# A hybrid attention layer's kernel, scheduled with and without the timeline simulation

## The chip, the cores and the metric

The kernel runs on one core of a Trainium2 chip. The metric is the device time of one execution in microseconds (us). A core has five engines with a queue each, which run in order within the queue and wait for one another by semaphores: PE (TensorE, matrix products; the profile lists its weight loads apart as PEld), DVE (VectorE, elementwise work), ACT (ScalarE, copies, casts and activation functions), POOL (GpSimd) and SP (SyncE, which here issues most of the DMAs). SBUF is the core's working memory, PSUM the memory that PE writes its products to.

## The reference

One layer of a decoder: a mixer of three kinds of heads, then an MLP, all in float32, on 512 tokens of width 2048.

```python
def hybrid_layer(x, norm1_w, w_in, ..., w_out, norm2_w, w_up, w_down):
    h = rmsnorm(x, norm1_w)
    proj = h @ w_in
    ...
    y_sb = stick_breaking_attention(heads(sb_q), heads(sb_k), heads(sb_v))   # 6 heads of 128
    y_sc = sc_b * causal_depthwise_conv(sc_c * sc_h, sc_conv_w)              # 4 groups of 128
    y_gdn = gdn_mixer(gdn_qkv, gdn_z, gdn_a, gdn_b, ...)                     # 6 heads of 128
    y = jnp.concatenate([y_sb.astype(x.dtype), y_sc, y_gdn], axis=-1)
    x = x + y @ w_out
    h2 = rmsnorm(x, norm2_w)
    return x + jnp.square(jax.nn.relu(h2 @ w_up)) @ w_down                   # width 8192
...
return rmsnorm(x, final_norm_w)
```

The gated delta rule (GDN) in `gdn_mixer` solves, for each head and each block of tokens, a unit triangular system, and then carries a 128×128 state from block to block:

```python
t_mat = lax.linalg.triangular_solve(eye + m, jnp.broadcast_to(eye, m.shape),
                                    left_side=True, lower=True, unit_diagonal=True)
...
v_new = u_c - w_c @ state
o = q_c @ state + a_c @ v_new
state = state * jnp.exp(gl_c)[..., None, None] + jnp.swapaxes(k_c, -1, -2) @ v_new
```

## The kernel before

**How the products are made.** Each large product is split for precision: an operand x becomes hi (x rounded to fp32r) and lo (x − hi), and a product is three matmuls, hi·hi, hi·lo and lo·hi (`mm3`, lines 107 to 111). A weight tile is therefore loaded (SP's queue), cast by ACT to hi, and subtracted by DVE to lo before PE can use it. For the projections this is `wload` (line 97): raw, whi and wlo are tiles of 128×512 with four buffers each, and one such chunk feeds 12 matmuls of 512 columns in `gemm_chunk` (line 113). For the MLP it is `w_prep` (line 838) with `split` (lines 823 to 825): W has three buffers of 128×1024, and several of the W are first summed by DVE (L842) or by an accumulating DMA of POOL's queue (L848, L858), because both MLP halves use a Strassen-like scheme of seven products (`UP`, `DOWN`, lines 713 and 714).

**The stages.** First the projection of v and of the gates (lines 179 to 320). Then the GDN heads: `gdn_in(h)` makes a head's q, k, v by three projections, a short convolution and SiLU on DVE and ACT, and the block matrices; `gdn_base(h)` inverts the triangular matrices; `gdn_scan(h)` carries the state through four blocks. `gdn_gate` and `sc_group`, projections with little else, are written between them (lines 654 to 680). Then the six attention heads (`sb_qk`, `sb_attn`, lines 684 to 704), the output projection with the second norm (lines 713 to 797), the up half of the MLP in 32 groups (`up_pair`, line 888), whose results h are stored to DRAM (L943), and the down half (`unit`, line 996), which reads them back (L956). The end is the final norm.

**The solve.** In `gdn_base` the inverse of the 32×32 diagonal blocks is a loop on DVE with two operations a step, each reading what the one before wrote; 16 partitions (4 blocks of 4 diagonal pieces) work at a time:

```python
for i in range(31, 0, -1):
    n = 32 - i
    tv = t[:, :i * n].rearrange("p (a b) -> p a b", a=i)
    V.tensor_tensor(out=tv, in0=B[:, 0:i, i:i + 1].broadcast_to([16, i, n]), ...)                    # L436
    V.tensor_tensor(out=Y[:, 0:i, i:32], in0=Y[:, 0:i, i:32], in1=tv, op=ALU.subtract)               # L438
```

Its input and its result go through DRAM (sm, Bq and sy, Xc; SP's queue), and small matmuls, transposes and copies behind it put the full inverse together.

**What sets the order.** The program is written against a tile framework. It records every instruction with its dependencies, and when the `with tile.TileContext(...)` block closes, a scheduler puts each engine's instructions into the order of that engine's queue. Each instruction has a priority, by default its place in the program. `with tc.high_priority(n)` moves those inside n places forward: `WPRIO` = 400 for `wload`, `DPRIO` = 120 for `w_prep`, `APRIO` = 60 for the down half's loads of h, `CPRIO` = 2000 for `gdn_base` and `gdn_scan` (lines 33 to 36, 645 to 652). The scheduler takes, for an engine that is free, the instruction of the highest priority among those that are ready. In this kernel the context is made with `schedule_with_timeline_sim=True` (line 1151): what is free and what is ready follows a simulation of the program's timeline. The order is fixed at compile time; on the chip each queue runs as written.

## Time and profile before

| | us |
|---|---|
| median of 2 runs | 2193.46 (2193.19 to 2193.73) |
| the profiled execution | 2195.19 |
| its span, first to last instruction | 2193.2 |
| HBM read, written | 302.94 MB, 45.48 MB |

The profiled execution is 1.7 us slower than the median of the runs. Its span is 2.0 us shorter than its time. The granted TensorE clock was 0.996 on the mean. In a group of the profile, "L104 DVE TENSOR_TENSOR wlo<-raw,whi ... x98 | 66.9, 683 | 5.7" is: line 104, engine DVE, operation, the tile written and those read, 98 instructions, 66.9 us busy in all, 683 ns each on the mean, and 5.7 us in which the engine stood idle just before them. A row of a view by stretches of time has for each engine its busy time and its instructions in that stretch, and then the mean granted clock, the busy share of the DMA engines and GB/s. A row of waits has the waiting engine and line, what it waited for, the time in all, the times and the longest.

The stages stand in the trace at about these times after the span's start: the first projection to 67 us, the GDN heads from there to 540, the attention heads to 755, the output projection to 913, the up half to 1555 and the down half to the end.

### The profile page before, as it was taken

Reading aid. Unit: us, or ns where it says so; the run is one execution under the profiler, and the core shown is the slowest. Engines: PE = TensorE matmul, PEld = TensorE weight load, DVE = VectorE, ACT = ScalarE, POOL = GpSimd, SP = SyncE. Lnnn points to the kernel's source line nnn. Section 1 sums busy time; section 2 is a strip of 40 time slices with the busy share of each in tenths; the row PEclk is TensorE's granted clock in tenths of the full one; section 3 lists DMA queues with packets and bytes.
Section 4 is the critical chain, followed back from the end, with each engine's and each line's share of the span. In section 5 each row is a group of like instructions: output and inputs, shape, how many; then the busy total and the mean of one; then the engine's idle time right before and its main releaser. Section 6 shows DMA issues by size and latency. Waiting matters only on the chain.

```text
span 2193.2 us, 33146 instructions
## 1 busy us (share of the span) xinstructions
PE 2153.2 (98%) x12698; PEld 1893.1 (86%) x12698; DVE 1695.1 (77%) x2335; ACT 1067.3 (49%) x1621; POOL 150.4 (7%) x203
## 2 busy tenths in 40 slices
PE   9999999999999999999999999999899999999998
PEld 8887787778989888799999999999788888888876
DVE  6689899754656755587788778877888898889884
ACT  6745566333434544444454445444454454445453
POOL 0000000000000011000000000000001000000113
PEclk9999999999999999999999999999999999999999
DMA  6332222222222344656665666666987777777762
GB/s 190 98 98 84 75 79 88 79 91 85 86 81 84 99 152 153 223 165 185 194 191 171 185 193 191 172 186 193 299 268 183 238 221 214 195 235 213 186 197 77
DMA packets 157390, 350.58 MB, mean 160 GB/s; under 512 B 19792, under 2 KB 59856, under 8 KB 157104
## 3 DMA queue, kind: packets, MB, share of 16 engines
q1 hardware_dynamic: 143984, 300.24, 40.6%
q0 software_dynamic: 13248, 48.24, 12.8%
q8 instruction: 99, 1.62, 0.3%
q14 instruction: 59, 0.48, 0.1%
HBM read 302.94 MB, written 45.48 MB: 159 GB/s over the span
## 4 chain that ended last, share of the span: by engine, by line
PE 91%; DVE 5%; DMA 1%; ACT 1%; issue 1%; SPq 0%; ACTq 0%; DVEq 0%
PE mm L110 10%; PE mm L109 10%; PE mm L111 10%; PE pu L111 10%; PE pu L109 10%; PE pu L110 10%; PE pp L110 8%; PE pp L111 8%; PE pp L109 8%; DVE wlo L104 1%; PE mm L274 1%; PE mm L272 1%; PE mm L273 1%; DVE W L825 1%; DVE Yq L438 1%
## 5 line engine op out<-in xcount | busy, mean ns | idle before, releaser
L824 ACT CAST W<-q 128x1024 fp32r<-128x1024 f32 x436 | 455.0, 1051 | 563.4 <-PE pp L111 247.1
L825 DVE TENSOR_TENSOR W<-q,W 128x1024 fp32r<-128x1024 f32 x436 | 530.5, 1225 | 121.6 <-ACT W L824 121.0
L109 PE MATMUL mm<-big,whi 128*128 128x512 f32 x1024 | 404.8, 396 | 1.8 <-DVE tmp L557 1.6
L111 PE MATMUL mm<-big,wlo 128*128 128x512 f32 x1024 | 403.8, 395 | 0.0
L110 PE MATMUL mm<-big,whi 128*128 128x512 f32 x1024 | 403.3, 394 | 0.0
L110 PE MATMUL pp<-W,A 128*128 128x512 f32 x840 | 328.0, 390 | 3.9 <-DVE W L825 3.9
L111 PE MATMUL pp<-W,A 128*128 128x512 f32 x840 | 327.4, 390 | 1.1 <-DVE A L825 1.1
L109 PE MATMUL pp<-W,A 128*128 128x512 f32 x840 | 325.6, 391 | 2.8 <-ACT A L824 2.8
L104 DVE TENSOR_TENSOR wlo<-raw,whi 128x512 fp32r<-128x512 f32 (+1 forms) x292 | 196.3, 674 | 146.5 <-ACT whi L103 133.7
L103 ACT CAST whi<-raw 128x512 fp32r<-128x512 f32 (+1 forms) x292 | 176.5, 605 | 267.6 <-PE mm L110 221.8
L111 PE MATMUL pu<-XS,W 128*128 128x256 f32 x1024 | 288.9, 282 | 1.2 <-DVE W L825 1.2
L109 PE MATMUL pu<-XS,W 128*128 128x256 f32 x1024 | 289.0, 282 | 1.0 <-ACT W L824 0.8
L110 PE MATMUL pu<-XS,W 128*128 128x256 f32 x1024 | 288.6, 282 | 0.0
L109 PEld LDWEIGHTS mm<-big,whi 128*128 128x128 f32 x1024 | 192.8, 188 | 40.6 <-DVE tmp L557 1.8
L111 PEld LDWEIGHTS mm<-big,wlo 128*128 128x128 f32 x1024 | 192.7, 188 | 40.0 <-DVE wlo L104 0.9
L110 PEld LDWEIGHTS mm<-big,whi 128*128 128x128 f32 x1024 | 192.8, 188 | 38.7 <-DVE big L723 0.3
L109 PEld LDWEIGHTS pu<-XS,W 128*128 128x128 f32 x1024 | 193.4, 189 | 2.0 <-ACT W L824 1.6
L111 PEld LDWEIGHTS pu<-XS,W 128*128 128x128 f32 x1024 | 193.4, 189 | 1.7 <-DVE W L825 1.7
L110 PEld LDWEIGHTS pu<-XS,W 128*128 128x128 f32 x1024 | 193.3, 189 | 0.0
L842 DVE TENSOR_TENSOR q<-q 128x1024 f32<-128x1024 f32 x156 | 190.2, 1219 | 2.1 <-DMA q<-in_wd_dram 0.7
L110 PEld LDWEIGHTS pp<-W,A 128*128 128x128 f32 x840 | 158.1, 188 | 38.4 <-DVE W L825 5.6
L109 PEld LDWEIGHTS pp<-W,A 128*128 128x128 f32 x840 | 158.0, 188 | 37.3 <-ACT A L824 4.1
(300 smaller groups left out, 3398.1 us busy)
## 6 DMA issues: line engine op xcount, KB each, us to landing
q<-in_wu_dram SPq DMA_DIRECT2D x128, 512.0 KB
q<-in_wd_dram SPq DMA_DIRECT2D x128, 512.0 KB
raw<-in_wa_dram SPq DMA_DIRECT2D x192, 256.0 KB
hs<-h SPq DMA_DIRECT2D x32, 1024.0 KB
q<-in_wd_dram POOLq DMA_DIRECT2D x60, 512.0 KB, 7.7
ha<-hs SPq DMA_DIRECT2D x56, 512.0 KB
raw<-in_wo_dram SPq DMA_DIRECT2D x64, 256.0 KB
q<-in_wu_dram POOLq DMA_DIRECT2D x32, 512.0 KB, 5.5
```

The costliest lines, as they stand in the source:

```text
L103: S.copy(out=hi[:, :n], in_=raw[:, :n])
L104: V.tensor_tensor(out=lo[:, :n], in0=raw[:, :n], in1=hi[:, :n].bitcast(F32), op=ALU.subtract)
L109: PE.matmul(p, lhsT=lh, rhs=rh, start=first, stop=False, skip_group_check=more)
L110: PE.matmul(p, lhsT=lh, rhs=rl, start=False, stop=False, skip_group_check=more)
L111: PE.matmul(p, lhsT=ll, rhs=rh, start=False, stop=last, skip_group_check=more)
L272: PE.matmul(o, lhsT=xw[k][:, 0, s], rhs=hi[:, ws], start=k == 0 and b % 2 == 0, stop=False)
L273: PE.matmul(o, lhsT=xw[k][:, 0, s], rhs=lo[:, ws], start=False, stop=False)
L274: PE.matmul(o, lhsT=xw[k][:, 1, s], rhs=hi[:, ws], start=False, stop=k == KT - 1 and b % 2 == 1)
L438: V.tensor_tensor(out=Y[:, 0:i, i:32], in0=Y[:, 0:i, i:32], in1=tv, op=ALU.subtract)
L824: S.copy(out=o[:, 0], in_=src)
L825: V.tensor_tensor(out=o[:, 1], in0=src, in1=o[:, 0].bitcast(F32), op=ALU.subtract)
L842: on_v = lambda t, u: V.tensor_tensor(out=t, in0=t, in1=u, op=ALU.add)
```

## The change

The context is made without the timeline simulation. The scheduler orders the instructions by their priorities alone, without its own model of their times. The instructions, their operands, tiles, buffer counts and priorities are the same.

```diff
-    with tile.TileContext(nc, schedule_with_timeline_sim=True) as tc:
+    with tile.TileContext(nc, schedule_with_timeline_sim=False) as tc:
```

## The prediction

> **What bounds the kernel now.** I read the page's first two parts, then busy time by stage, then groups and timeline where the engines are fullest.
>
> ```profile
> span 2193.2 us, 33146 instructions
> PE 2153.2 (98%) x12698; PEld 1893.1 (86%) x12698; DVE 1695.1 (77%) x2335; ACT 1067.3 (49%) x1621; POOL 150.4 (7%) x203
> ...
> PE   9999999999999999999999999999899999999998
> ...
> DVE  6689899754656755587788778877888898889884
> ...
> PEclk9999999999999999999999999999999999999999
> ```
>
> TensorE is busy for 2153.2 of 2193.2 us. All its idle time is 2193.2 − 2153.2 = 40.0 us, that is 1.8%. No order takes a matmul away, so the room for a gain is about these 40 us. DVE is full in two places, slices 3 to 8 and the last quarter. The next view gives the busy time by stage: the GDN heads, the attention heads, the output projection, the MLP's up and down halves.
>
> ```profile
> 110.00:450.00 340.00, 330.30 (x1711) 268.10 (x1710) 300.66 (x691) 179.62 (x375) 13.03 (x32) 0.99 0.28 84
> ...
> 550.00:755.00 205.00, 205.00 (x1148) 179.76 (x1146) 133.18 (x186) 93.84 (x159) 6.97 (x20) 1.00 0.26 81
> 755.00:913.00 158.00, 158.00 (x749) 131.57 (x748) 88.51 (x129) 73.70 (x127) 20.24 (x15) 1.00 0.51 159
> 913.00:1555.00 642.00, 636.98 (x5334) 634.92 (x5333) 512.82 (x639) 315.96 (x422) 28.80 (x33) 1.00 0.65 189
> 1555.00:2193.00 638.00, 620.34 (x2717) 509.23 (x2715) 543.53 (x488) 298.82 (x322) 73.12 (x75) 0.99 0.72 210
> ```
>
> The columns are PE, PEld, DVE, ACT, POOL, then clock, DMA share and GB/s. In 550:913 PE is busy for every microsecond and DVE for 221.7 of 363, so an order that is less exact has slack there. The GDN stage 110:450 has the least: DVE works 300.66 of 340 us (88%) and PE 330.30. What DVE does there:
>
> ```profile
> L104 DVE TENSOR_TENSOR wlo<-raw,whi 128x512 fp32r<-128x512 f32 x98 | 66.9, 683 | 5.7 <-ACT whi L103 4.4
> L438 DVE TENSOR_TENSOR Yq<-Yq,tq 16x60 f32<-16x60 f32 (+15 forms) x186 | 62.8, 338 | 4.9
> L436 DVE TENSOR_TENSOR tq<-Bq,Yq 16x60 f32<-16x60 f32 (+15 forms) x186 | 62.8, 338 | 10.7 <-DMA Bq<-sm 6.1
> L342 DVE SCALAR_TENSOR_TENSOR cv<-xp,vc,cv 128x512 f32<-128x512 f32 x39 | 29.3, 751 | 1.5 <-ACT cv L340 1.0
> ```
>
> The two lines of the solve in gdn_base (L436, L438: 31 + 31 operations for each of 6 heads, each operation reading what the one before wrote) take 125.6 us, 20.9 us a head. The wlo of L104 is what PE needs: one for every 12 matmuls of a projection. The solve runs under high_priority(2000), wlo under 400, the convolution (L342) under none. The timeline of DVE shows how they are ordered now:
>
> ```profile
> 121.01 0.26 DVE L438 TENSOR_TENSOR Yq<-Yq,tq 16x112 f32<-16x112 f32 x1
> 121.30 0.29 DVE L436 TENSOR_TENSOR tq<-Bq,Yq 16x135 f32<-16x135 f32 x1
> 121.62 0.29 DVE L438 TENSOR_TENSOR Yq<-Yq,tq 16x135 f32<-16x135 f32 x1
> ...
> 122.82 0.75 DVE L342 SCALAR_TENSOR_TENSOR cv<-xp,vc,cv 128x512 f32<-128x512 f32 x1 [0.22 <-ACT cv L340]
> 123.49 0.32 DVE L436 TENSOR_TENSOR tq<-Bq,Yq 16x175 f32<-16x175 f32 x1
> 123.74 0.73 DVE L342 SCALAR_TENSOR_TENSOR cv<-xp,vc,cv 128x512 f32<-128x512 f32 x1
> 124.40 0.32 DVE L438 TENSOR_TENSOR Yq<-Yq,tq 16x175 f32<-16x175 f32 x1
> 124.65 0.67 DVE L104 TENSOR_TENSOR wlo<-raw,whi 128x512 fp32r<-128x512 f32 x1
> ```
>
> This carries the argument. A solve step of priority 2000 is followed by a convolution step of no priority, that by a solve step, that by a wlo. An order by priorities alone does not give this: each solve step needs only its predecessor on the same engine, so all 62 would go first. The timeline simulation gives it because, in its picture, a step's result is not there yet when the engine comes free, and a lower instruction fills the place.
>
> **The change part by part.** It adds no instruction and removes none, and no duration changes. It moves instructions within each engine's queue.
>
> *The solve.* I take the solve as one unbroken run on DVE. Its length: a dependent step starts 0.03 us after its predecessor's end (121.01 + 0.26 = 121.27, next at 121.30; 121.59, next at 121.62), while an independent one starts 0.07 us before it (123.74 + 0.73 = 124.47, next at 124.40). So 20.9 + 62 × 0.03 = 22.8 us. The Trainium skill, "VectorE: DVE Perf Modes", section "The DRAIN you can't avoid", says that the next DVE operation waits until the pipe is empty, with or without a semaphore between them; by that the run would be no longer than the mixed one's parts and the sum below 11 us less. The rows do not agree (+0.03 against −0.07), and I go by the rows.
>
> While DVE is in that run, no wlo is made. Behind the run stand wlo, the convolutions and the PSUM evacuations; raw is freed by wlo, so the loads on SP's queue wait too. PE lives on the chunks already split. Their time comes from a stretch where PE is full:
>
> ```profile
> 770.00:825.00 55.00, 55.00 (x256) 45.59 (x255) 30.80 (x44) 25.34 (x43) 6.80 (x5) 1.00 0.52 162
> ```
>
> 55 / 256 = 0.215 us a matmul, 2.6 us a chunk of 12. The wlo tile has bufs=4, so at most 4 chunks, 10.3 us, are ready; between solves DVE has slack, so I take the whole 10.3. PE then stands for 22.8 − 10.3 = 12.5 us a head, 75 us for six. Bounds: PE has 1711 − 98 × 12 = 535 small matmuls in the stage that need no wlo; at most a tenth of a microsecond each, about 9 us a head, could fill the hole (3.5 us a head, 21 in all). With only 2 chunks ready it is 17.6 us a head, 106 in all.
>
> *The clock after a stall.* Here is what such a hole does today, and what the hand-over at 913 us does:
>
> ```profile
> 260.00:265.00 5.00, 2.69 (x42) 1.97 (x42) 4.88 (x12) 2.24 (x8) 0.00 (x0) 0.95 0.25 83
> 265.00:270.00 5.00, 4.05 (x19) 3.21 (x18) 4.70 (x9) 4.39 (x9) 0.11 (x1) 0.50 0.01 3
> 270.00:275.00 5.00, 5.00 (x21) 3.93 (x21) 4.73 (x8) 2.93 (x6) 0.10 (x1) 0.87 0.00 2
> ...
> 880.00:935.00 55.00, 50.21 (x290) 43.64 (x289) 32.91 (x42) 26.13 (x41) 5.17 (x4) 0.97 0.67 220
> ```
>
> The granted clock falls to 0.50 behind a hole: 5 × (0.05 + 0.50 + 0.13) = 3.4 us of full speed lost in the first, 55 × 0.03 = 1.65 us in the second. Six holes cost 10 us at 1.65 (20 at 3.4).
>
> *What comes back.* PE's idle time in 110:450 is 9.7 us; I take it as time in which PE waits for steps of a head's chain, solve included. A run of 23 us instead of a mixed one delivers these sooner. I give back all of it, 10 us (bounds 0, and 14 with some 4 us of such waits after 450).
>
> *The other stages.* In the MLP both halves are rows of weight splits:
>
> ```profile
> L825 DVE TENSOR_TENSOR W<-q,W 128x1024 fp32r<-128x1024 f32 x436 | 530.5, 1225 | 121.6 <-ACT W L824 121.0
> ...
> L842 DVE TENSOR_TENSOR q<-q 128x1024 f32<-128x1024 f32 x156 | 190.2, 1219 | 2.1 <-DMA q<-in_wd_dram 0.7
> ```
>
> The longest dependent pair there is one add and one split, 2.4 us. One W feeds 24 matmuls, 24 × 642 / 5334 = 2.9 us in the up half and 24 × 638 / 2717 = 5.6 us in the down half, and W has three buffers. Two of them ahead hide the pair: cost 0. If that cover went once for each of the 32 groups of the up half, it would be 32 × 1.22 = 39 us. SP's queue is in order and full of waits:
>
> ```profile
> SPq L100 <- DVE wlo L104: 530.6, 214, 13.6
> ...
> SPq L943 <- DVE h L738: 374.1, 31, 13.1
> ```
>
> A store of h already holds the loads behind it for 374.1 / 31 = 12 us, and PE is full all the same, since a group lasts 642 / 32 = 20 us. POOL's queue, which issues the accumulating loads, is busy 7% of the span. I cost both queues at 0; a load that came a whole store later would cost what is left of 12 us once the 2.9 us of the W in hand are gone.
>
> **Sum.** 75 + 10 − 10 = +75 us on the profiled execution's 2195.2 us; the median of the runs is 2193.46, 1.7 us below it. 2193.5 + 75 = 2268 us. By the bounds of this case: 21 + 10 − 14 = +17 (2210) to 106 + 20 − 0 = +126 (2320).
>
> **The rivals.**
> *Nearly the same order (on the other side: not slower).* The argument names one simulation; without it the library still orders along some simulation of its own, and if that one also lets a step's result come later than its engine, the solve stays mixed as in the rows at 122.82 to 124.65. Then the queues change only locally, the cost is a few waits of the size of those in 110:450 (up to 9.7 us more) or less: 2185 to 2210, say 2197. It decides as soon as a wlo gets onto DVE every 10.3 us. For it speaks that buffer counts tie the loads down whatever the order; against it that DVE's 88% leaves little room for another order.
> *No picture of time at all.* Then PE's queue too has a head's whole chain in one piece, and PE waits out every step. The solve's 22.8 us are exposed in full, and of the scan, for each of 4 blocks, one operation from each row:
>
> ```profile
> L503 ACT ACTIVATE vn<-s,be 128x128 f32<-128x128 f32 x24 | 8.7, 361 | 14.5 <-PE s L501 14.3
> ...
> L501 PE MATMUL s<-bp,MT 128*128 128x128 f32 x36 | 7.7, 295 | 1.5 <-DVE bp L498 1.5
> L506 PE MATMUL s<-vn,kdec 128*128 128x128 f32 x36 | 7.3, 285 | 0.4 <-ACT vn L503 0.4
> L496 PE MATMUL s<-Sn,kq 128*128 128x128 f32 x36 | 7.2, 282 | 0.6 <-ACT Sn L509 0.6
> ...
> L498 DVE SCALAR_TENSOR_TENSOR bp<-s,negeg,y 128x128 f32<-128x128 f32 x18 | 6.1, 341 | 5.5 <-PE s L496 5.4
> ...
> L511 DVE SCALAR_TENSOR_TENSOR Sn<-Sn,elast,s 128x128 f32<-128x128 f32 x12 | 4.1, 345 | 3.2 <-PE s L506 3.0
> ```
>
> That is 1.9 us a block, 7.6 a head: 6 × (22.8 + 7.6) = 182 us or more, 2375 and up. Against it: the change takes one model of times away, and a queue with no picture of any kind would leave PE with nothing between the steps of a chain, which is a far larger step than one argument's name tells.
> *The MLP loses its cover.* The 39 us above: 2232.
> *Faster.* The unbroken chains take all 40 us of idle time away: 2153. It needs the hand-overs at 913 and 1555 to close too, 5.0 and 17.7 us of it, which have nothing to do with the solve.
>
> **How the numbers follow.** Chances: unbroken solve 0.45 (2268; a seventh of it under 2237), nearly the same 0.38, no picture of time 0.08, the MLP's cover 0.06 (half under 2237), faster 0.03. The measurement tells about 2%, 44 us, from no change: faster is under 2150, slower over 2237. Faster 0.03; same 0.38 + 0.07 + 0.03 = 0.48 less 0.02 for a larger local loss, 0.46; slower 0.51. The likeliest case is 2268, its own range 2210 to 2320. The range of all must take in the second case and leaves out the third and the gain: 2185 to 2320.
>
> **What would show it.** In the changed profile the timeline of DVE between 110 and 550 us has L436 and L438 alternating 62 times with nothing between; PE idle before "mm" ended by "DVE wlo L104", some 12 us six times; PEclk digits below 9 in slices 3 to 10; 550 us onward shifted as a block, the MLP's two halves as long as now. I am wrong if L104 rows still stand between solve rows, if the GDN stage keeps its length, or if the added time lies behind 913 us.

## The result, and the profile after

The changed kernel takes 2213.36 us (median of 2 runs, 2211.27 to 2215.46) where the one before took 2193.46. The ratio is 1.0087, with a 95% interval of 1.0071 to 1.0103: a small loss of 0.9%, clearly above zero and within the 2% that count as no change. The forecast was 2268 us with a range of 2185 to 2320: the direction and the range hold, the size does not (20 us in place of 75), and the cause that the prediction took for the likeliest is not the one that the trace shows.

The page of the changed kernel, its first two parts, then the chain that ended last and the group of the projections' third matmul:

```profile
span 2213.5 us, 33135 instructions
...
PE 2165.4 (98%) x12698; PEld 1891.4 (85%) x12698; DVE 1695.2 (77%) x2335; ACT 1072.8 (48%) x1621; POOL 153.4 (7%) x203
...
PEclk9999999999999999999999999999999999999999
...
PE 85%; DVE 9%; ACT 2%; DMA 2%; issue 2%; SPq 0%; POOL 0%; ACTq 0%; DVEq 0%; POOLq 0%
...
L111 PE MATMUL mm<-big,wlo 128*128 128x512 f32 x1024 | 407.7, 398 | 8.8 <-DVE wlo L104 8.8
```

The same two lines of the page of the kernel before:

```profile
PE 91%; DVE 5%; DMA 1%; ACT 1%; issue 1%; SPq 0%; ACTq 0%; DVEq 0%
...
L111 PE MATMUL mm<-big,wlo 128*128 128x512 f32 x1024 | 403.8, 395 | 0.0
```

DVE's work is the same to 0.1 us (1695.1 and 1695.2), but its share of the chain that sets the end has gone from 5% to 9%, and a wait of PE for wlo that did not exist is now 8.8 us. PE's idle time is 2213.5 − 2165.4 = 48.1 us, 8.1 more than before. That is less than half of the 20.3 us by which the span has grown. The rest does not show as idle time. The mean granted clock has gone from 0.996 to 0.993, which is (0.007 × 2213.5) − (0.004 × 2193.2) = 6.7 us of full speed. The last 5.5 us are what is left; I take them to lie in matmuls that stand in the queue with their records overlapping, so that PE looks busy while it starts fewer of them. That is argued, not measured.

Busy time by stage of the changed kernel, with the columns as in the prediction. The bounds are moved to where the stages now end:

```profile
110.00:450.00 340.00, 323.87 (x1667) 253.93 (x1668) 290.89 (x671) 176.37 (x370) 14.10 (x33) 0.98 0.25 78
...
547.00:761.00 214.00, 207.03 (x1143) 177.93 (x1142) 133.29 (x187) 93.80 (x160) 8.21 (x24) 1.00 0.25 78
761.00:933.50 172.50, 172.50 (x788) 141.62 (x787) 92.97 (x133) 75.85 (x130) 18.94 (x14) 1.00 0.46 151
933.50:1580.00 646.50, 643.00 (x5384) 641.40 (x5384) 517.29 (x645) 322.46 (x427) 30.27 (x34) 1.00 0.64 189
1580.00:2213.00 633.00, 618.10 (x2714) 509.47 (x2712) 543.93 (x487) 298.79 (x322) 75.20 (x75) 0.99 0.73 212
```

In 110:450 PE starts 1667 matmuls where it started 1711, and DVE does 671 operations where it did 691: the loss begins here. In the attention stage PE was busy for all of 550:755; now 214.00 − 207.03 = 7.0 us are idle. In both MLP halves PE's idle time has shrunk a little (3.5 us against 5.0, 14.9 against 17.7). By the first matmul of each, the up half begins at 907.3 us before and at 933.5 after, 26.2 us later; it then lasts 646.5 us where it lasted 648.1, and the down half with the end 633.5 where it lasted 637.8. So 26.2 us are lost ahead of the MLP, and 5.9 come back in it. Of the 26.2 some 7 are the attention heads' idle time, and most of the rest, 19, lies in the GDN heads.

Now the two places. First the timeline of DVE in the changed kernel, at the first head's solve and then where the first two heads' solves meet (an x2 row is two operations in a row from the same line, one of each head, under the shape of the first):

```profile
121.20 0.29 DVE L436 TENSOR_TENSOR tq<-Bq,Yq 16x135 f32<-16x135 f32 x1
121.52 0.29 DVE L438 TENSOR_TENSOR Yq<-Yq,tq 16x135 f32<-16x135 f32 x1
121.74 0.41 DVE L399 TENSOR_TENSOR MT<-i,g 128x256 f32<-128x256 f32 x1
122.07 0.30 DVE L436 TENSOR_TENSOR tq<-Bq,Yq 16x156 f32<-16x156 f32 x1
...
134.99 0.67 DVE L104 TENSOR_TENSOR wlo<-raw,whi 128x512 fp32r<-128x512 f32 x1
135.59 0.40 DVE L436 TENSOR_TENSOR tq<-Bq,Yq 16x252 f32<-16x252 f32 x1
...
140.27 0.36 DVE L438 TENSOR_TENSOR Yq<-Yq,tq 16x207 f32<-16x207 f32 x1
140.66 0.58 DVE L436 TENSOR_TENSOR tq<-Bq,Yq 16x192 f32<-16x192 f32 x2
141.27 0.59 DVE L438 TENSOR_TENSOR Yq<-Yq,tq 16x192 f32<-16x192 f32 x2
...
148.59 0.57 DVE L438 TENSOR_TENSOR Yq<-Yq,tq 16x60 f32<-16x60 f32 x2
...
149.30 0.67 DVE L104 TENSOR_TENSOR wlo<-raw,whi 128x512 fp32r<-128x512 f32 x1
```

At 121.74 an operation of another line still stands between two steps of one solve. So one solve alone still leaves gaps, and others fill them; I take it that the scheduler has not lost every picture of time. What is new is at 140.66. The end of head 0's solve and the beginning of head 1's run side by side, and each fills the other's gaps, so that no place is left for a wlo. None is made from the end of the one at 134.99 (135.7) to 149.30, 13.6 us. The first 5.0 us of this are not the double run: from 135.59 to 140.63 twelve steps of head 0 alone follow one another with nothing between, although ACT had the next whi ready at 136.8 (L103, 136.14 + 0.62). So for these twelve steps DVE does what the prediction expected of all 62.

In the kernel before, the timeline of DVE shows the same two heads side by side, too:

```profile
153.19 0.55 DVE L438 TENSOR_TENSOR Yq<-Yq,tq 16x156 f32<-16x156 f32 x2
153.77 0.69 DVE L337 TENSOR_TENSOR xp<-mm,R 128x512 f32<-128x512 f32 x1
154.38 0.55 DVE L436 TENSOR_TENSOR tq<-Bq,Yq 16x135 f32<-16x135 f32 x2
154.96 0.69 DVE L104 TENSOR_TENSOR wlo<-raw,whi 128x512 fp32r<-128x512 f32 x1
155.57 0.55 DVE L438 TENSOR_TENSOR Yq<-Yq,tq 16x135 f32<-16x135 f32 x2
```

There a lower instruction stood behind most double steps, a wlo among them. The chain that ended last, of the changed kernel (start, duration, what), shows what the missing place costs, and the waits in 110:550 how often:

```profile
148.59 0.22 DVE Yq L438
...
148.83 0.34 DVE Yq L438
...
149.37 0.61 DVE wlo L104
149.99 0.04 issue
150.03 0.50 PE mm L111
```

```profile
PE mm L111 <- DVE wlo L104: 8.8, 2, 4.5
...
PE o L533 <- DVE MT L530: 3.6, 3, 1.3
PE b L452 <- DVE X L447: 3.6, 2, 3.4
```

The chain runs through steps of both solves, through one wlo, and only then back to PE. There are two such holes, 4.5 us at most and 8.8 in all: one from 145.7 to 150.0, where the solves of heads 0 and 1 meet, and one from 338.5 to 343.0, where those of heads 3 and 4 do. At the second meeting no wlo is made from 330.7 to 342.2, 11.5 us, and the double run is 7.2 of them. Before it the casts were missing, too: ACT made no whi from 327.6 to 335.5, since its queue stood before a step of another chain (L130) that waited for DVE's L541, and then three in a row from 335.50 on. A wlo behind the first of these would still have come before PE ran dry at 338.5 (335.50 + 0.62 + 0.69 = 336.8 by the durations of the rows); the double run left no place for it. The third row is a hole of 3.4 us that ends at 466: the base matmuls of L452 stand ahead of other work while their input (Xc, read back from DRAM) is still under way. Stretches of 5 us with the granted clock around the three:

```profile
145.00:150.00 5.00, 0.70 (x2) 0.27 (x2) 4.56 (x17) 0.00 (x0) 0.00 (x0) 1.00 0.00 0
150.00:155.00 5.00, 4.97 (x15) 3.94 (x16) 4.57 (x10) 0.62 (x1) 1.09 (x2) 0.66 0.59 175
340.00:345.00 5.00, 2.03 (x5) 1.65 (x6) 4.69 (x15) 0.00 (x0) 0.00 (x0) 0.68 0.18 56
345.00:350.00 5.00, 5.00 (x16) 3.94 (x15) 4.10 (x10) 0.62 (x1) 1.09 (x2) 0.63 0.69 193
465.00:470.00 5.00, 3.86 (x38) 2.83 (x39) 0.74 (x2) 1.14 (x3) 0.00 (x0) 0.50 0.33 105
470.00:475.00 5.00, 5.00 (x30) 3.32 (x29) 1.56 (x4) 0.95 (x3) 0.00 (x0) 0.85 0.17 52
```

Behind each hole the clock is low: 5 × (0.34 + 0.32 + 0.37 + 0.50 + 0.15) = 8.4 us of full speed, beside 12.2 us for the three holes themselves. That is an upper bound, since the clock is already at 0.50 for about 1 us at the end of the second and the third hole, where PE has nothing to do. In the first row PE is busy for 0.70 of 5 us, DVE for 4.56.

The second place is the attention stage. Of the waits there in the changed kernel, these two have no counterpart before:

```profile
PEld z L622 <- ACT zs L614: 7.7, 6, 1.6
...
PE z L622 <- ACT zs L614: 5.7, 5, 1.4
```

Each of the six heads' transposes (L622) now stands on PE's queue before the softmax (L602 to L614) has delivered, while projection matmuls that need nothing of it stand behind. Six weight loads wait, and five of the matmuls behind them.

### The profile page after: what moved, and what is told of

The parts are those of the page before. It is cut to its first block, busy times and chain, and to the rows that moved or that the text cites. A ratio compares the mean times of both kernels' runs of the same rounds, so it can differ in the third digit from the quotient of the medians.

```text
span 2213.5 us, 33135 instructions
## 1 busy us (share of the span) xinstructions
PE 2165.4 (98%) x12698; PEld 1891.4 (85%) x12698; DVE 1695.2 (77%) x2335; ACT 1072.8 (48%) x1621; POOL 153.4 (7%) x203
## 4 chain that ended last, share of the span: by engine, by line
PE 85%; DVE 9%; ACT 2%; DMA 2%; issue 2%; SPq 0%; POOL 0%; ACTq 0%; DVEq 0%; POOLq 0%
PE pu L109 10%; PE pu L111 10%; PE pu L110 10%; PE mm L111 9%; PE mm L110 9%; PE mm L109 9%; PE pp L111 8%; PE pp L109 8%; PE pp L110 8%; DVE Yq L438 2%; DVE tq L436 1%; DVE wlo L104 1%; DVE W L825 1%; DMA ha<-hs 1%; PE mm L274 0%
## 5 line engine op out<-in xcount | busy, mean ns | idle before, releaser
L103 ACT CAST whi<-raw 128x512 fp32r<-128x512 f32 (+1 forms) x292 | 176.6, 606 | 311.2 <-PE mm L110 266.0
```

The source lines that it names most:

```text
L103: S.copy(out=hi[:, :n], in_=raw[:, :n])
```

## The experiments

All are timed against the kernel before on the same chip. That kernel's median was 2193.96 to 2196.37 us in these sessions, so ratios are compared, and differences in us stand beside them.

**wlo ahead of the solve.** If the solves starve wlo because they stand above it, a higher priority for the weight split should close the holes.

```diff
-WPRIO = 400
+WPRIO = 4000
```

> The changed kernel with the projections' weight splits (wload) 4000 places forward in place of 400, so ahead of the solve's 2000. Theory (two heads' solves fill each other's gaps on DVE, wlo of lower priority gets no place, PE stands 4.3 and 4.5 us at 150 and 343 us and then runs at half clock): both holes go, with them 9 us of idle time and 3 to 5 us of half clock; 2199 to 2204 us, no PE row ended by DVE wlo L104 over 1 us. Rival (the extra time is spread over many small waits of a less exact order): within 4 us of 2213.

Measured: 2209.82 us (2207.85 to 2210.89), ratio 1.0071 (1.0056 to 1.0086), 3.5 us less than the changed kernel and 6 above the expected range. The waits for wlo are gone, but others are there, by the waits of this kernel in 67:560:

```profile
PE b L452 <- DVE X L447: 13.1, 4, 4.9
```

PE now stands before the base matmuls of L452 until 161.8 and 351.9 us, behind the same two meetings of solves. In the changed kernel these matmuls began at 161.2 and 354.5 us. So they come about when they did, and PE waits for them where it waited for wlo. The holes have changed their name. The starved wlo is one face of a DVE that has two solves to do at once; which of its consumers waits is a matter of priority.

**The solves of two heads kept apart.** The two heads use different partitions (0 and 32) of the same tiles. On the same partitions the second cannot begin before the first has ended and its result is stored.

```diff
-        p0 = 32 * (h % 2)
+        p0 = 0
```

> The changed kernel with all heads' solves on the same 16 partitions of Bq, Yq and tq, so that one head's solve cannot run beside the next one's. Theory of the two solves: no double run on DVE, the holes at 150 and 343 us go as in the run above, 2199 to 2206 us, unless a solve that has to wait for its predecessor makes a later hole. Rival (the single solve of priority 2000 is what starves wlo): the holes stay, 2211 us or more.

Measured: 2182.83 us (2182.51 to 2183.22), ratio 0.9949 (0.9933 to 0.9966). That is 30.5 us less than the changed kernel and 11 less than the kernel before, and 16 us below the expected range. The steps of head 0 that ran closed up in the changed kernel, with head 1's behind them, have places for wlo again, at 137.44, 140.03 and 142.79:

```profile
137.44 0.67 DVE L104 TENSOR_TENSOR wlo<-raw,whi 128x512 fp32r<-128x512 f32 x1
```

The GDN stage of this kernel, then of the changed one, then of the one before, in the same 440 us:

```profile
110.00:550.00 440.00, 438.38 (x2295) 351.73 (x2294) 340.16 (x783) 220.29 (x452) 16.67 (x44) 1.00 0.27 86
```

```profile
110.00:550.00 440.00, 420.48 (x2136) 331.53 (x2137) 336.37 (x756) 207.32 (x431) 14.49 (x35) 0.98 0.26 81
```

```profile
110.00:550.00 440.00, 426.39 (x2203) 346.89 (x2202) 346.50 (x772) 213.03 (x445) 14.30 (x37) 0.99 0.28 85
```

PE's idle time there is 1.6, 19.5 and 13.6 us, the clock 1.00, 0.98 and 0.99. By the first matmuls the attention heads, the up half and the down half all begin 31 us earlier than in the changed kernel (516.1, 902.5 and 1549.0 us against 547.2, 933.5 and 1580.0): the whole gain lies in the GDN heads. The starts of matmuls tell it most plainly: 2295, 2136 and 2203.

The edit does a second thing. In the changed kernel, at a step of head 3, whose solve is on partitions 32 and up, the timeline of DVE has:

```profile
318.92 0.41 DVE L438 TENSOR_TENSOR Yq<-Yq,tq 16x255 f32<-16x255 f32 x1
319.36 0.69 DVE L104 TENSOR_TENSOR wlo<-raw,whi 128x512 fp32r<-128x512 f32 x1
320.09 0.41 DVE L436 TENSOR_TENSOR tq<-Bq,Yq 16x256 f32<-16x256 f32 x1
```

The wlo needs nothing of the step, and it begins 0.03 us after the step's end (318.92 + 0.41 = 319.33). Beside head 0's steps, on partitions from 0 on, it begins 0.07 us before the end (134.65 + 0.41 = 135.06, the wlo at 134.99). So DVE loses 0.10 us each time it goes from partitions from 0 on to those from 32 on, or back. Its rows show some 260 such places in the changed kernel and 215 in the kernel before, 26 and 22 us of its time by this estimate; with all solves on one set there are none beside their steps, and DVE's busy time falls from 1695.2 to 1678.6 us. The two orders share this cost to within 4 us, so it does not explain the loss of 20 us. But in the double runs each operation changes partitions (29 and 25 times, 3.0 and 2.6 us), so part of each hole is this. The 30.5 us are the price of both things together. A run with all solves on partitions 32 and up would part them; there is none.

**The softmax ahead.** For the attention's six waits the theory was that the softmax chain comes too late; moved forward, it should be done in time. Lines 602 to 614 went into a block, `...` standing for them:

```diff
+SPRIO = 600
...
+        with tc.high_priority(SPRIO):
...
```

> The changed kernel with the attention's softmax part (lines 602 to 614, DVE and ACT) 600 places forward, so ahead of wlo and of the next head's splits. Theory (PE reaches the transposes of zs 1.0 to 1.4 us too early in six heads, since L613 stands behind one wlo and one sq split on DVE): the six waits for ACT zs L614, 5.7 us on PE and 7.7 on PEld, go down to under 2 us in all; 2206 to 2209 us. Rival (the order puts the transposes where its own picture has exp done, so a chain that is moved forward takes the transposes along): the waits stay at 1 us a head, 2211 to 2215 us.

Measured: 2212.56 us (2210.27 to 2217.95), ratio 1.0088 (1.0073 to 1.0103): nothing gained. The waits stay (the line numbers have moved by 2):

```profile
PE z L624 <- ACT zs L616: 7.4, 6, 1.3
```

A miss. An earlier softmax makes the transposes ready earlier too, in the scheduler's picture, and they stand before it on PE's queue as they did. What is early or late by itself was not the cause; the order of the transposes against the projections was.

**Both of these.** WPRIO = 4000 and the softmax block together.

> The edits of the first and the third run together. Theory: the gains add, 2192 to 2198 us, level with the kernel before. Rival (each edit only shuffles the order): no better than the better of the two.

Measured: 2207.5 us (2205.49 to 2209.24), ratio 1.0061 (1.0046 to 1.0076). The expected sum of gains is missed: the priorities do not win the loss back, alone or together.

**The solves apart, without the change.** To see whether the gain above belongs to the new order or to the edit, the same edit in the kernel before:

```diff
-        p0 = 32 * (h % 2)
+        p0 = 0
```

> The kernel before, so with the timeline simulation, with all heads' solves on the same 16 partitions. Theory (the simulation of the kernel before already put wlo between the two solves where they overlap, at 152 to 162 us, so the overlap costs there little): within 6 us of 2194, so that with the solves apart the change itself is no loss, or a gain of 5 us and more. Rival (the overlap of two solves is bad under any order, and the single set is worth 30 us everywhere): 2160 to 2170 us, and the change still costs some 20 us.

Measured: 2188.6 us (2186.66 to 2189.84) beside 2196.37, ratio 0.9962 (0.9948 to 0.9976). The edit is worth 7.8 us under the timeline simulation and 30.5 without it. Once the solves are on one set of partitions, the two orders are alike: 0.9962 and 0.9949, with intervals that overlap. So the change itself is no loss; it becomes one through what the second set allows, the side-by-side solves.

**The transposes later.** The reverse of the softmax experiment: the second part of an attention head, from the transposes to its output (L617 to L642), goes 150 places back, on top of the solves apart.

```diff
-        p0 = 32 * (h % 2)
+        p0 = 0
...
+        with tc.high_priority(-150):
             wb = [xps("z") for _ in range(3)]
...
             ys[h] = y
```

> The changed kernel with the solves on one set of partitions, and the second part of the attention (transposes of zs, splits of hl, product with v) 150 places back, so that the next head's projection goes ahead of it on PE. Theory (PE stands 1.0 to 1.4 us before the transposes in six heads, because it has been put ahead of work that is ready): the six waits for ACT zs L614 go, 2175 to 2178 us. Rival (the scheduler's picture places transposes exactly when its exp is done whatever their priority, or there is no other ready work): the waits stay, 2181 to 2185 us, or the moved part comes late and costs more.

Measured: 2175.88 us (2175.44 to 2176.96) beside 2196.37, ratio 0.9907 (0.9892 to 0.9922). Of PE's five waits there one is left in 500:760:

```profile
PE z L623 <- ACT zs L614: 0.5, 1, 0.5
```

This is the fastest version of all, 6.9 us better than with the solves apart alone by the medians and 9 by the ratios; the waits came to 5.7 us on PE. It is faster than both kernels, by 0.9% and 1.7%.

**Another number for the priority.** Is the loss a draw, one unlucky order of many? With CPRIO = 1900 for 2000 the solves still stand above all else, so a cause should stay and a draw might not.

```diff
-CPRIO = 2000
+CPRIO = 1900
```

> The changed kernel with 1900 in place of 2000 for base and scan, an edit without a purpose: it shows how far the time depends on details of the order. Theory (the loss has a cause of its own, two solves side by side): same double runs and holes, 2209 to 2217 us. Rival (the 20 us are one draw among many orders): anything between 2180 and 2230, with holes elsewhere.

Measured: 2213.62 us (2212.25 to 2214.94), ratio 1.0078 (1.0063 to 1.0093). The same double rows on DVE, the same two holes. This is a weak test of a draw, since the number left the order nearly as it was; that the loss has a cause rests on the runs that keep the solves apart.

**Order of the program alone.** A way to see the unbroken solve, and an order with no picture of time: the framework keeps the order in which the program is written.

```diff
-    with tile.TileContext(nc, schedule_with_timeline_sim=False) as tc:
+    with tile.TileContext(nc, schedule_with_timeline_sim=False, linearize=True) as tc:
```

> The changed kernel with the scheduler told to keep the program's own order on each engine: no picture of time and no priority at work. By the prediction's third rival each head's chain is exposed in full: 2375 us and more. The solve then runs unbroken, 62 steps, and shows the length that the prediction gave it (22.8 us) and the hole that it gave for it (12.5 us a head).

Measured: 10079.49 us. A miss for the price: here the instructions follow one another across the engines too, one at a time, which is another thing than six exposed chains, and its time says nothing on the rival. But it holds what I wanted to see, the solve in one piece. The first and the last row of the first one, in the timeline of DVE:

```profile
395.26 0.19 DVE L436 TENSOR_TENSOR tq<-Bq,Yq 16x31 f32<-16x31 f32 x1 [11.33 <-POOL Yq L432]
...
417.64 0.18 DVE L438 TENSOR_TENSOR Yq<-Yq,tq 16x31 f32<-16x31 f32 x1
```

62 steps from 395.26 to 417.82, 22.6 us, where the prediction had 22.8. It is the likeliest case's own run; the changed kernel has no run of 62, only one of twelve, before the first double run.

**One of the two meetings.** Head 1 alone on the other partitions: the pair of heads 0 and 1 can still meet, 3 and 4 cannot.

```diff
-        p0 = 32 * (h % 2)
+        p0 = 32 * (h == 1)
```

> The changed kernel with a second set of partitions for head 1 alone: only the solves of heads 0 and 1 can overlap. Theory (each pair of solves side by side has its own price): the hole at 150 us and its half clock stay, the one at 343 us goes, and the time falls between the changed kernel and the one with all solves apart, 2193 to 2203 us. Rival (the single set helps by another way, through the order as a whole): at one of the two ends, under 2187 or over 2209.

Measured: 2197.38 us (2195.9 to 2203.4), ratio 1.0023 (1.0013 to 1.0033), 16 us below the changed kernel and 14.5 above the version with all solves apart. The waits of this kernel in 110:547 have one hole left:

```profile
PE mm L111 <- DVE wlo L104: 4.3, 1, 4.3
```

It is the one at 149 us; that at 343 is gone. So the hole of a meeting comes and goes with the meeting, and the two prices, some 15 us each, add up. They are more than the holes (4.3 and 4.5 us) and the low clock behind them (at most 1.7 and 3.5). The hole that ended at 466 has gone with the second meeting, and the first set of partitions now holds heads 3 and 5 as well, so the second price has their changes of partitions in it.

**The late transposes without the change.** Both edits of the fastest version, in the kernel before.

> The kernel before, with the timeline simulation, and both edits of the best version (solves on one set, second part of the attention 150 places back). Theory (the six waits before the transposes are not there under the timeline simulation, so moving them back gains nothing): 2185 to 2192 us, so the version without the timeline simulation stays ahead by 10 us. Rival (the two edits are good under any order): 2178 us or less.

Measured: 2187.74 us (2186.78 to 2189.09) beside 2194.02, ratio 0.9972 (0.9962 to 0.9981). Under the timeline simulation the late transposes bring nothing over the solves apart (0.9962). So with its order put right by hand in two places, the kernel without the simulation is ahead by 0.65% (0.9907 and 0.9972; about 12 us by the medians, 14 by the ratios).

## Why the prediction was right or wrong

**Where it failed: "I take the solve as one unbroken run on DVE."** The argument was that an order by priorities gives no gaps, since a step needs only its predecessor. The row at 121.74 contradicts it: something of lower priority still stands between two steps, as the rival "nearly the same order" had it. The longest run of one solve's steps with nothing between is twelve, not 62. The term of 75 us rests on this sentence. The prices in it were right, or nearly: 22.8 us for the run (22.6 in the program's order), and 10.3 us for PE's cover (at the first hole the last wlo ends at 135.7 and PE runs dry at 145.7, 10.0 us; at the second 330.7 and 338.5, 7.8 us, since the casts were late). What was wrong is where and how often DVE is shut for longer than that: 13.6 us (135.7 to 149.3) and 11.5 us (330.7 to 342.2), where two solves meet, and not 22.8 us six times. So there are two holes of 4.4 us, 8.8 in all, and not six of 12.5, 75 in all.

**The rival "nearly the same order".** Its premise was right and its price was nearly right: the solve stays mixed, 2185 to 2210 against 2213.4. Its condition, that it decides as soon as a wlo gets onto DVE every 10.3 us, pointed at the right place, but it is not sharp. The changed kernel also has 10.6 and 10.4 us without a wlo (from 286.3 and 303.8), and the version with the solves apart 12.7 and 12.1 (from 412.1 and 156.4), without a hole over 1 us there: PE then had chunks enough in hand, or matmuls of a base or a scan among those of the projections. I had looked at one solve. That two of them can meet stood in the trace of before (the x2 rows at 153.19); that in another order they would shut DVE did not.

**The clock.** 1.65 to 3.4 us a hole, 10 us for six. Right in kind: the three stretches shown lose at most 1.7, 3.5 and 3.3 us (8.4 in all), the upper end of what was taken for a hole. With three holes, not six, and with the holes of before gone, 6.7 us are left of the 10 by the mean clocks.

**What comes back.** The 10 us were wrong. Nothing came back: PE's idle time in the GDN stage rose, from 13.6 to 19.5 us in 110:550, and where nearly all of it goes, down to 1.6, the solves are on one set of partitions.

**The other stages.** "An order that is less exact has slack there", said of the attention heads and the output projection, was half wrong: the output projection is as full as before, but the attention heads lose 7 us, most of it in the waits before the transposes. DVE's free time is no measure of slack for a queue that is in order: PE's queue had a waiting instruction ahead of ready ones. The run with the late transposes prices these waits at 6.9 us. For the MLP the zero was right, and the rival that it loses its cover fell: both halves have less idle time on PE than before.

**No picture of time, and faster.** The first did not happen, and no run here prices it. A gain from this change alone did not happen either; with the two edits the new order gives 0.9907.

**The rule on the pipe of DVE.** The Trainium skill, "VectorE: DVE Perf Modes", "The DRAIN you can't avoid", says that the next operation does not start until the pipe is empty, and adds that one that is not held starts earlier; the prediction left the addition out. The rows agree with the addition. The unbroken run has 62 steps in 22.6 us and 20.5 us of busy time, 0.03 us from one step to the next, while the wlo at 134.99 ends at 135.66 and the next step starts at 135.59. So a dependent step waits, and an independent operation does not, as the prediction read it. What it missed is the third case: an independent one waits, too, where the partitions change (the wlo at 319.36).

**What stays open.** Why the two solves fill each other's gaps wholly in the one order and leave places behind double steps in the other, and why twelve steps of head 0 close up ahead of the first double run: the scheduler's own times are not in a trace. How much of the gain from one set of partitions is the end of the meetings and how much the end of the changes of partitions was not tried. And the hole at 466 us was not tried by itself; it is gone in the versions with the solves apart.

## What to carry to other kernels

A long chain of small dependent steps with a high priority did no harm on a shared engine here as long as its gaps were open; two such chains at once closed each other's gaps and shut out all that stood below. Look in the trace for places where two chains run side by side, and measure the longest time in which the engine makes nothing for the bottleneck against the number of buffers between them and the other work that the bottleneck has there. If it is too long, keep the chains apart by a shared buffer: here priorities only chose who waited. And look at the partitions: a chain on other partitions than the work around it cost DVE 0.10 us at each change.

## What the runs showed of the hardware

The granted clock does not need an empty PE to fall. In the kernel before with the solves apart, stretches of 5 us at the end of the GDN stage:

```profile
480.00:485.00 5.00, 3.08 (x14) 2.25 (x15) 2.33 (x4) 2.07 (x7) 0.00 (x0) 0.74 0.16 54
485.00:490.00 5.00, 3.97 (x17) 3.38 (x17) 3.35 (x6) 3.04 (x6) 0.10 (x1) 0.50 0.03 5
490.00:495.00 5.00, 5.00 (x18) 3.98 (x18) 5.00 (x10) 0.89 (x2) 0.00 (x0) 0.74 0.30 103
```

PE is busy for 3.08 of 5 us with small matmuls of a scan that wait for one another, with no single gap over some 0.9 us, and the clock goes to half for some 10 us all the same: 5 × (0.26 + 0.50 + 0.26) = 5.1 us of full speed at most, since PE also waits in part of it. A chain of short waits can cost about as much as a hole that catches the eye.
